# A two-layer encoder trunk on one core: keys that stay unnormalised until the block inverse, reordered transfers, and small matrix products spread over four tiles of TensorE

## The chip, the core and the metric

The kernel runs on one core of a Trainium2 chip. The core has TensorE (PE, matrix products into PSUM), VectorE (DVE), ScalarE (ACT), GpSimd (POOL) and a queue engine (SP); ACT and SP start transfers here. The metric is the device time of one execution in microseconds (us), as the median of several.

## What is computed

The input is one sequence of 1024 rows of 1024 float32 numbers. It passes an even layer (gated mixing and trailing means), a SwiGLU feed-forward block, an odd layer (RWKV-7 time mixing), a second SwiGLU block and a last norm. The part that the change touches most is the odd layer:

```python
r = xr @ w_r
k = xk @ w_k
kk = heads(k * k_k)                                  # 16 heads of 64
kk = kk / jnp.maximum(jnp.sqrt(jnp.sum(kk * kk, axis=-1, keepdims=True)), 1e-12)
...
y = wkv7_scan(rh, decay, kh, vh, -kk, kk * ah)       # a recurrence over the 1024 steps
...
def swiglu(hn, w_gate, w_up, w_down):
    return (jax.nn.silu(hn @ w_gate) * (hn @ w_up)) @ w_down
```

The recurrence multiplies a 64 by 64 state per head by its decay, adds a rank-one correction made of the normalised keys, and adds value times key.

## The kernel before, in words

**Numbers.** A dense product in float32 is made of three products of fp32r operands (high by high, high by low, low by high). Each weight block of 128 by 1024 is loaded by ACT's queue into `raw`, copied to `whi` by ACT and subtracted to `wlo` by DVE (L157 and L158, helper `split`); the three products are L399 to L401 (`mm3`). Small products are plain float32 and take two TensorE passes each.

**Halves.** The sequence is cut in two halves A and B of 512 columns (`h` = 0, 1), and a dense product streams 512 columns. The first layer and its feed-forward block run first. The gate and up products leave their hidden values in DRAM (`hid_d`), and the down products read them back (`hd`, L894). `down_steps` (L883) loads one group of two or three hidden blocks ahead; half A's groups alternate between a set of slots called `low` (tiles `ahi`, `alo`) and three slots `hd`. The residual of half A, `H[0]`, and of half B, `H[1]`, come back from `hm_d` (L1885, L1891).

**Projection, once for each half** (`project`, L1180). It runs over eight pairs of heads, p = 0 to 7. For each p: the key product, two low-rank products, the receptance product `r`, the square sums of the keys by four products with two columns (`norms`, into `bo`), a square root on POOL (`rsqrt`, L404), eight products that spread the result over the rows (`rb`, L1333), the keys times that (`kkn`, L1339), and from these the tiles `ar` and `bk` that go to DRAM. One p later `interact` (L1233) makes the 64 by 64 interactions of eight chunks, sixteen products (L1238); they go to DRAM, and after p = 3 and p = 7 a tile `iat` with 128 blocks of 32 by 32 comes back. `invert` (L1402) turns these into inverses in 31 steps on DVE, which are handed out five at a time between the other work. Gate values `g_d` are written from two tags of two buffers (L1212, L1214).

**Recurrence, once for each half** (`recur`, L1440), eight chunks of 64 steps, beside the dense products of a feed-forward block. For each chunk, `load` fetches `ar`, `bk`, `uv` and the inverse blocks `XT`; `gram` (products of `ar` with `bk`), `flip_bk` (transposes), `below` and `below2` (32 by 32 products that fill the lower block of the inverse), `own`, the product with `XT`, the state and the output follow. `bk` has one buffer, so the next chunk's load waits for `flip_bk`. All products of `recur` go through one helper, so most have line L1460.

**Order of the work.** Each engine runs its instructions in a fixed order, which the framework's scheduler sets by a simulated timeline; `drive` and `beside` set how side work is handed out between dense products, `tc.issue_after` puts one instruction behind another on its queue. A transfer on SP also waits until the transfer that used its completion semaphore before, some eight transfers back, has ended.

**The end.** Half A of the second block runs groups of hidden blocks `G1A`; after blocks 18 and 19 and their down products come the output projection of half B (`out_proj`), its norm, blocks 20 and 21, and then half B's feed-forward block.

Of the kernel before, what the change touches and what calls it, by code (L numbers as in the profile page):

```python
# [16 lines left out]
P = 128  # L17
# [11 lines left out]
LOWRANK_AT, GATE_AT, MIX_AT = (2, 8), (3, 8), (1, 2)  # L29
# [14 lines left out]
def tile_trunk(  # L44
# [309 lines left out]
    push_ffn(1, 0, G1A[2], push_act(("y", 1), y_d[1]))  # L354
    for e in push_o(1):
        e()
    push_ffn(1, 0, G1A[3])
# [525 lines left out]
    def down_steps(h, groups, wslot, hslot, ahead=True, after=None, between=iter(()), at={}, first={}):  # L883

        held = {}
# [4 lines left out]
        def load(g):  # L890
            for f in g:
                if f not in held:
                    held[f] = hslot(f)
                    sp.dma_start(held[f].bitcast(F32), hid_d[h][:, f])  # L894
# [38 lines left out]
    def ffn(l, h, hn, fp, groups=GROUPS, last=False, nd=3, after=None, between=iter(()), early=False):  # L933
# [3 lines left out]
        for kind, f in ffn_events(groups, early):  # L937
# [27 lines left out]
            else:  # L965
# [6 lines left out]
                for m in range(KT):  # L972
# [7 lines left out]
                    yield len(f) / 8  # L980

# [63 lines left out]
    xi_d = [dram.tile([2, 8, 2, 8, 32, 2, 32], F32, name=f"xi_d{h}") for h in range(2)]  # L1045
    at_d = [dram.tile([2, 8, 2, 8, 32, 32], F32, name=f"at_d{h}") for h in range(2)]
# [137 lines left out]
    def project(h, hn1, kp, ring, keep, before_v):  # L1184
# [21 lines left out]
        for m in range(KT):  # L1206
# [4 lines left out]
            t = tmp(("epx", "k")[m % 2], 2)  # L1211
# [21 lines left out]
        def interact(p, ar, bk):  # L1233

            oa = auxt()
            for c in range(8):
                for r in range(2):
                    pe.matmul(  # L1238
                        oa[rows[r], c * 64 : (c + 1) * 64], bk[rows[r], c, 0, :], ar[rows[r], c, 0, :],
                        start=True, stop=True,  # L1240
                    )
            at = tmp("kkn", 2)
            act.activation(at, oa, AF.Copy)
# [6 lines left out]
            if p % 4 == 3:  # L1250
                iat = tmp("iat", 1, [P, 32, 32])
                for q in range(2):
                    sp.dma_start(
                        iat[q * 64 : q * 64 + 64].rearrange("b s t -> b (s t)"),
                        at_d[h][q, p - 3 : p + 1].rearrange("p r c s t -> (p r c) (s t)"),
                    )
                return iat

        def bonus(p, kt, j):
            pe.matmul(  # L1260
                bo[:, j * 16 + 2 * p : j * 16 + 2 * p + 2], kt[:, j * P : (j + 1) * P], ind2, start=True, stop=True
            )

# [13 lines left out]
        for p in range(KT):  # L1277
# [32 lines left out]
            n2 = bo[:, 64 + 8 * p : 72 + 8 * p]  # L1310
            rn = tmp("rn", 2, [P, 4, 2, 8])[:, 0, 0, :]

            def norms(j):
                pe.matmul(n2[:, 2 * j : 2 * j + 2], sq[:, j * P : (j + 1) * P], ind2, start=True, stop=True)
                if j == 3:
                    dve.tensor_scalar(out=rn, in0=n2[:, 0:8], scalar1=1e-24, scalar2=None, op0=ALU.max)
                    rsqrt(rn)

            small = [lambda j=j: norms(j) for j in range(4)]
            if prev is not None:  # L1320
                small += [lambda j=j, pv=prev: bonus(pv[0], pv[3], j) for j in range(4)]
            if p:
                o = mmt()
                dense2(o, *take(("r", h, p)), xr, between=small)
            else:
                o = o_r
                for go in small:
                    go()
            invert_on(INV)
            rb = auxt()  # L1330
            for j in range(4):
                for r in range(2):
                    pe.matmul(  # L1333
                        rb[rows[r], j * P : (j + 1) * P], bc(rn[:, 2 * j + r : 2 * j + r + 1], [P, 64]), ident,
                        start=True, stop=True,
                    )
# [696 lines left out]
```

## Time and profile before

| what | value |
|---|---|
| median of 3 executions | 2438.87 us (2436.91 to 2441.32) |
| the profiled execution, its own time | 2432.77 us |
| span in its profile | 2431.1 us |
| mean granted TensorE clock | 0.987 |
| PE matmul busy | 2347.3 us, 97% |
| DVE busy | 1475.1 us, 61% |
| ACT busy | 937.1 us, 39% |
| POOL busy | 214.8 us, 9% |
| moved by DMA | 342.17 MB, 141 GB/s |

A group row of the profile reads: line, engine, operation, written tile and read tiles, shapes, count, busy time and the mean length of one, then the idle time of the engine just before the group and what ended it. Because matmuls are pipelined, the lengths of neighbours overlap: the busy time of a group divided by its count is what one pass really takes. A row of stretches gives, after the stretch, the busy time of each engine with its count, the granted clock, the share of the DMA engines and GB/s.

### The profile page before, as it was taken

The page shows a single profiled execution, that of the slowest core. Times are in us where ns is not written, and L with a number is a line of the kernel's source. Part 1 is how long each engine was busy: PE and PEld are TensorE (multiplying, and loading weights), DVE is VectorE, ACT ScalarE, POOL GpSimd, SP SyncE. Part 2 cuts the span into 40 slices and gives each one's busy share as a digit, 9 for nine tenths or more (in the row PEclk, how much of TensorE's full clock was granted, in tenths as well). Part 3 has the DMA queues.
Part 4 walks back from the last instruction along what each step waited for, and adds up shares of the span by engine and source line. Part 5 has one row for each costly group of instructions (what it writes and reads, how often), then busy time and mean ns, then how long its engine had stood idle before and what let it go on. Part 6 is the DMA issues. An engine that isn't in the chain of part 4 may idle for free. (4 is left out here: it accounts for less than half of the span.)

```text
span 2431.1 us, 38203 instructions
## 1 busy us (share of the span) xinstructions
PE 2347.3 (97%) x15567; PEld 1917.3 (79%) x15567; DVE 1475.1 (61%) x2328; ACT 937.1 (39%) x1403; POOL 214.8 (9%) x246
## 2 busy tenths in 40 slices
PE   8999999999899999999999999999999999999998
PEld 6888888888687878777777778777878788888887
DVE  6445765655567857856767947866664536444443
ACT  6233444444214753423335744433332224322223
POOL 0200000000000033201100123201100001000001
PEclk9999999999999999999999999999999999999999
DMA  5114443324665565775435465675544423433231
GB/s 179 52 52 147 152 152 96 121 96 165 226 233 172 171 163 133 207 202 167 143 117 168 150 169 142 190 232 159 146 121 132 123 77 97 144 98 96 86 105 52
DMA packets 406767, 342.17 MB, mean 141 GB/s; under 512 B 78080, under 2 KB 351616, under 8 KB 405824
## 3 DMA queue, kind: packets, MB, share of 16 engines
q10 hardware_dynamic: 266048, 195.33, 27.0%
q1 hardware_dynamic: 140544, 144.41, 19.1%
q8 instruction: 122, 2.00, 0.3%
q14 instruction: 53, 0.43, 0.1%
HBM read 263.07 MB, written 76.61 MB: 140 GB/s over the span
## 5 line engine op out<-in xcount | busy, mean ns | idle before, releaser
L399 PE MATMUL mm<-ahi,whi 128*128 128x512 f32 x1376 | 541.0, 394 | 7.0 <-ACT whi L157 3.0
L400 PE MATMUL mm<-alo,whi 128*128 128x512 f32 x1376 | 541.7, 394 | 2.6 <-DVE alo L158 2.5
L401 PE MATMUL mm<-ahi,wlo 128*128 128x512 f32 x1376 | 539.7, 392 | 1.6 <-DVE wlo L158 1.6
L157 ACT ACTIVATE whi<-raw 128x1024 fp32r<-128x1024 f32 (+1 forms) x280 | 282.1, 1014 | 572.2 <-PE mm L400 441.7
L158 DVE TENSOR_TENSOR wlo<-raw,whi 128x1024 fp32r<-128x1024 f32 (+1 forms) x280 | 328.5, 1177 | 249.8 <-ACT whi L157 231.5
L399 PEld LDWEIGHTS mm<-ahi,whi 128*128 128x128 f32 x1376 | 258.7, 188 | 66.2 <-ACT whi L157 4.7
L400 PEld LDWEIGHTS mm<-alo,whi 128*128 128x128 f32 x1376 | 258.8, 188 | 60.6 <-DVE alo L158 5.6
L401 PEld LDWEIGHTS mm<-ahi,wlo 128*128 128x128 f32 x1376 | 258.7, 188 | 57.9 <-DVE wlo L158 2.9
L493 DVE TENSOR_TENSOR h<-h,mm 128x512 f32<-128x512 f32 x276 | 185.8, 684 | 149.4 <-PE mm L401 148.4
L399 PE MATMUL mm<-hidhi,wdhi 128*128 128x512 f32 x304 | 118.4, 398 | 3.2 <-ACT hidhi L958 2.5
L400 PE MATMUL mm<-hidlo,wdhi 128*128 128x512 f32 x304 | 120.0, 395 | 0.0
L401 PE MATMUL mm<-hidhi,wdlo 128*128 128x512 f32 x304 | 119.7, 394 | 0.0
L730 PE MATMUL mm<-ahi,whi 128*128 128x512 f32 x296 | 115.6, 390 | 0.0
L731 PE MATMUL mm<-alo,whi 128*128 128x512 f32 x296 | 115.2, 389 | 0.0
L732 PE MATMUL mm<-ahi,wlo 128*128 128x512 f32 x296 | 113.6, 389 | 0.0
L955 DVE TENSOR_TENSOR sg<-sg,mm 128x512 f32<-128x512 f32 x52 | 35.7, 687 | 119.8 <-PE mm L401 119.6
L157 ACT ACTIVATE wdhi<-raw 128x1024 fp32r<-128x1024 f32 x42 | 43.3, 1056 | 160.2 <-PE mm L400 137.0
L399 PE MATMUL mm<-hd,dhi 128*128 128x512 f32 x192 | 75.9, 396 | 13.8 <-DMA hd<-hid_d 11.4
L400 PE MATMUL mm<-hd,dhi 128*128 128x512 f32 x192 | 75.8, 395 | 0.0
L401 PE MATMUL mm<-hd,dlo 128*128 128x512 f32 x192 | 74.9, 393 | 0.0
L399 PEld LDWEIGHTS mm<-hidhi,wdhi 128*128 128x128 f32 x304 | 57.7, 190 | 16.5 <-ACT hidhi L958 2.9
L400 PEld LDWEIGHTS mm<-hidlo,wdhi 128*128 128x128 f32 x304 | 57.9, 190 | 12.3 <-issue 0.5
(395 smaller groups left out, 4274.2 us busy)
## 6 DMA issues: line engine op xcount, KB each, us to landing
raw<-in_ffn_w_down_dram ACTq DMA_DIRECT2D x88, 512.0 KB
raw<-in_ffn_w_gate_dram ACTq DMA_DIRECT2D x74, 512.0 KB
raw<-in_ffn_w_up_dram ACTq DMA_DIRECT2D x74, 512.0 KB
hid_d<-hid SPq DMA_DIRECT2D x36, 512.0 KB
hd<-hid_d SPq DMA_DIRECT2D x26, 512.0 KB
raw<-in_ab_w_in_dram ACTq DMA_DIRECT2D x16, 512.0 KB
raw<-in_ab_w_out_dram ACTq DMA_DIRECT2D x16, 512.0 KB
raw<-in_rwkv_w_r_dram ACTq DMA_DIRECT2D x16, 512.0 KB
```

Of the source, the lines that this page charges most:

```text
L157: act.activation(hi, src, AF.Copy)
L158: (eng or dve).tensor_tensor(out=lo, in0=src, in1=hi.bitcast(F32), op=ALU.subtract)
L399: pe.matmul(o, whi, xhi, start=first, stop=False)
L400: pe.matmul(o, whi, xlo, start=False, stop=False)
L401: pe.matmul(o, wlo, xhi, start=False, stop=last)
L493: dve.tensor_tensor(out=H[h][:, m, :], in0=H[h][:, m, :], in1=o, op=ALU.add)
L730: pe.matmul(o, wh[:, k, :], x[0][:, k, :], start=st, stop=False, skip_group_check=True)
L731: pe.matmul(o, wh[:, k, :], x[1][:, k, :], start=False, stop=False, skip_group_check=True)
L732: pe.matmul(o, wl[:, k, :], x[0][:, k, :], start=False, stop=k == 3, skip_group_check=True)
L955: dve.tensor_tensor(out=s, in0=s, in1=o, op=ALU.mult)
```

## The change

1. **Keys.** `kkn` becomes the unnormalised key times its factor, one ACT copy with a scale. The root on POOL and the `rb` products are gone. The inverse square norms enter later: `sums` takes the square sums of four p from `bo`, transposes them (one product), writes them to `n2_d`, and `interact` reads them back into row 31 of `iat`, takes the reciprocal and multiplies the 31 other rows; `invert` starts from a diagonal of these numbers and not of ones.
2. **Four tiles.** `interact` sends odd chunks to the other half of the output rows and to a second PSUM bank, with two ACT copies for one. `below` and `below2` do the same with 32 by 32 products: pairs of odd p go to the other 32 columns. `w1` is one ACT copy for an ACT and a DVE copy, the copies to `XT` are four for two, and `load` fetches a small tile `xo` twice per chunk.
3. **Transfers.** In the first down products the hidden blocks of the next group come ahead of the rest of `H[0]` and `H[1]`, `hd` has four slots, and half B's groups are loaded ahead. `lnw` comes behind the keys of chunk 2. The state goes through DRAM between the halves. The gate values use four tags.
4. **Order.** Half B's low-rank product is taken at event 6 and not 8. At the end, groups 20 and 21 are joined with 18 and 19, so the gate product of block 20 comes ahead of the down products of 18 and 19.

```diff
-LOWRANK_AT, GATE_AT, MIX_AT = (2, 8), (3, 8), (1, 2)
+LOWRANK_AT, GATE_AT, MIX_AT = (2, 6), (3, 8), (1, 2)
...
                 wd = {f: take(("d", 0, h, f)) for f in g}
+                if ahead and gi + 1 < len(groups):
+                    load(groups[gi + 1])
                 if gi in at:
                     at[gi]()
-                if ahead and gi + 1 < len(groups):
-                    load(groups[gi + 1])
...
-            t = tmp(("epx", "k")[m % 2], 2)
+            t = tmp(("k", "epx", "av", "sg")[m % 4], 2)
...
-            oa = auxt()
+            oa = [auxt() for _ in range(2)]
             for c in range(8):
+                e, i = c % 2, c // 2
                 for r in range(2):
                     pe.matmul(
-                        oa[rows[r], c * 64 : (c + 1) * 64], bk[rows[r], c, 0, :], ar[rows[r], c, 0, :],
+                        oa[e][rows[r ^ e], i * 64 : (i + 1) * 64], bk[rows[r], c, 0, :], ar[rows[r], c, 0, :],
...
+                dve.tensor_scalar(out=d2, in0=d2, scalar1=1e-24, scalar2=None, op0=ALU.max)
+                dve.reciprocal(d2, d2)
+                dve.tensor_tensor(out=iat[:, 0:31], in0=iat[:, 0:31], in1=bc(d2.unsqueeze(1), [P, 31, 32]), op=ALU.mult)
...
+        def sums(p):
+
+            rn = tmp("rn", 1, [P, 64])[:, :32]
...
+            ot = auxt()
+            pe.transpose(ot[:32, :P], rn, ident)
+            t = nt.tile([P, HT], F32, tag="nsq", bufs=2, name="n2")[:32, :P]
+            act.activation(t, ot[:32, :P], AF.Copy)
+            for q in range(2):
+                sp.dma_start(
+                    n2_d[h][q, p - 3 : p + 1].rearrange("p r (j c) t -> (p r j) c t", c=2),
...
-            rb = auxt()
-            for j in range(4):
-                for r in range(2):
-                    pe.matmul(
-                        rb[rows[r], j * P : (j + 1) * P], bc(rn[:, 2 * j + r : 2 * j + r + 1], [P, 64]), ident,
-                        start=True, stop=True,
-                    )
...
-            dve.scalar_tensor_tensor(out=kkn, in0=kt, scalar=col(C_KK + p), in1=rb, op0=ALU.mult, op1=ALU.mult)
+            act.activation(kkn, kt, AF.Copy, scale=col(C_KK + p))
...
-        pool.memset(xf[:, 0:2048:65], 1.0)
+        dve.tensor_copy(xf[:, 0:2048:65], iat[:, 31, :])
...
+                sp.dma_start(xo[b0 : b0 + 32], x2[:, 1::2, :])
+                loaded[0] = sp.dma_start(XT[b0 + 32 : b0 + 64, :, 32:64], x2)
...
             for p in range(8):
                 for r in (1, 0):
+                    b0, o0 = r * 64, r * 64 + 32 * (1 - p % 2)
+                    mm(
+                        ow[o0 : o0 + 32, p // 2, 0:32], gt[b0 : b0 + 32, p, r, 32:64], x1[b0 : b0 + 32, p, :],
+                        start=True, stop=True, tile_position=(b0, o0),
+                    )
...
-                    with tc.issue_after(loaded[0].ins):
+                    with tc.issue_after(loaded[0].ins), tc.issue_after(keys[0].ins):
...
-    wslot, hslot = slots_of(f, 4, 3)
+    wslot, hslot = slots_of(f, 4, 4)
...
-    for k in range(4, KT, 2):
-        a_loaded = sp.dma_start(H[0][:, k : k + 2, :], hm_d[0][:, k : k + 2, :])
...
+    def rest_a():
+        for k in range(4, KT, 2):
+            with tc.issue_after(hid_loads[-1]):
+                sp.dma_start(H[0][:, k : k + 2, :], hm_d[0][:, k : k + 2, :])
...
-    drive(ffn(1, 0, hnA, f, G1A[2], between=take_act(("y", 1)), early=True))
-    exhaust(out_proj(1, ys))
-    hnB = norm_split(1, C_FFN + 8, b)
-    drive(ffn(1, 0, hnA, f, G1A[3], last=True, early=True))
+    drive(ffn(1, 0, hnA, f, G1A[2] + G1A[3], last=True, between=take_act(("y", 1)), early=True, then={G1A[2][0][-1]: out_b}))
```

On SP, at the passage from the first block's gate and up products to half A's down products, before (`hid_d` ends in 77 for half A and 78 for half B, `h<-hm_d_75` is `H[0]`, `h<-hm_d_76` is `H[1]`, `hd` is the second group):

```order
L743 DMA hid_d_77<-hid 128x1024
L743 DMA hid_d_78<-hid 128x1024
L1885 DMA h<-hm_d_75 128x1024 x2
L1891 DMA h<-hm_d_76 128x1024 x4
L894 DMA hd<-hid_d_77 128x1024 x3
L894 DMA ahi<-hid_d_77 128x1024
L894 DMA alo<-hid_d_77 128x1024
```

And at the same place of the changed kernel:

```order
L747 DMA hid_d_77<-hid 128x1024
L747 DMA hid_d_78<-hid 128x1024
L898 DMA hd<-hid_d_77 128x1024 x3
L1913 DMA h<-hm_d_75 128x1024 x2
L898 DMA hd<-hid_d_77 128x1024
L898 DMA ahi<-hid_d_77 128x1024
L898 DMA alo<-hid_d_77 128x1024
L1926 DMA h<-hm_d_76 128x1024 x2
L898 DMA hd<-hid_d_77 128x1024 x2
```

The three `hd` loads of the second group moved from behind six loads of `h` to the front of them.

On SP, at the start of half A's recurrence, before (from the residual of half B, `h`, by way of the second chunk's `ar`, `uv` and, for each half of the rows, two loads into `XT`, to its `bk`):

```order
L1791 DMA h<-h_d_86 128x1024 x4
L1475 DMA ar<-ar_d_1974 128x1024
L1480 DMA uv<-v_d_1978 64x512
L1481 DMA uv<-v_d_1978 64x512
L1487 DMA XT<-xi_d_1984 32x8x64
L1490 DMA XT<-xi_d_1984 32x8x32
L1487 DMA XT<-xi_d_1984 32x8x64
L1490 DMA XT<-xi_d_1984 32x8x32
L1477 DMA bk<-bk_d_1976 128x1024
```

And in the changed kernel:

```order
L1820 DMA h<-h_d_86 128x1024 x4
L1495 DMA ar<-ar_d_1974 128x1024
L1500 DMA uv<-v_d_1978 64x512
L1501 DMA uv<-v_d_1978 64x512
L1508 DMA XT<-xi_d_1984 32x8x64
L1511 DMA xo<-xi_d_1984 32x4x32
L1512 DMA XT<-xi_d_1984 32x8x32
L1508 DMA XT<-xi_d_1984 32x8x64
L1511 DMA xo<-xi_d_1984 32x4x32
L1512 DMA XT<-xi_d_1984 32x8x32
L1497 DMA bk<-bk_d_1976 128x1024
```

The second chunk's `bk` stands where it stood, with two `xo` loads more ahead of it, and two more in the first chunk's loads.

On PE, in half A's projection, at the end of a receptance product, before (`kkn` squares and `k` bonus sums go into `bo`, `rn` is what the `rb` products spread):

```order
L400 MATMUL mm<-xlo,whi 128x512
L401 MATMUL mm<-xhi,wlo 128x512
L1260 MATMUL bo<-ind_6460,k 128x2 x4
L1333 MATMUL aux<-ident,rn 64x128 x8
L399 MATMUL mm<-xhi,whi 128x512
```

And in the changed kernel:

```order
L404 MATMUL mm<-alo,whi 128x512
L405 MATMUL mm<-ahi,wlo 128x512
L1349 MATMUL bo<-ind_6461,kkn 128x2 x4
L1276 MATMUL bo<-ind_6461,k 128x2 x4
L403 MATMUL mm<-xhi,whi 128x512
```

The eight `rn` rows are gone, and the two groups of four products into `bo`, which stood some twenty dense products apart, stand together.

More of the change, by code (lines that the diff above doesn't have):

```diff
@@ L353, in tile_trunk @@
     push_ffn(1, 0, G1A[1])
[L354 to L357, printed above, removed]
+    y1, o1 = push_act(("y", 1), y_d[1]), push_o(1)
+    for i, e in enumerate(e for e in ffn_events(G1A[2] + G1A[3], True) if e[0] != "d"):
+        if e == ("u", G1A[3][0][0]):
+            for go in o1:
+                go()
+        push_ffn_event(1, 0, *e)
+        if e[0] in "gu":
+            next(y1, None)
     push_ffn(1, 1)
@@ L881, in full_steps, with down_steps @@
             yield 0.5
-    def down_steps(h, groups, wslot, hslot, ahead=True, after=None, between=iter(()), at={}, first={}):
-        held = {}
+    def down_steps(h, groups, wslot, hslot, ahead=True, after=None, between=iter(()), at={}, first={}, loaded=None):
+        held, loaded = {}, [] if loaded is None else loaded
         for g in groups:
@@ L930, in slots_of, with ffn @@
         )
-    def ffn(l, h, hn, fp, groups=GROUPS, last=False, nd=3, after=None, between=iter(()), early=False):
+    def ffn(l, h, hn, fp, groups=GROUPS, last=False, nd=3, after=None, between=iter(()), early=False, then={}):
         dests["d"] = lambda: (fp.tile([P, D], F32R, tag="wdhi", bufs=nd, name="wdhi"),
@@ L1242, in interact @@
             at = tmp("kkn", 2)
-            act.activation(at, oa, AF.Copy)
+            for e in range(2):
+                act.activation(c64(at)[:, e::2, :], c64(oa[e][:, :256]), AF.Copy)
             for r in range(2):
@@ L1309, in project @@
             pool.tensor_copy(pct[:, h * 8 : h * 8 + 8, p], c64(epx)[:, :, 63])
[L1310 to L1321, printed above, removed]
+            n2 = bo[:, 64 + 8 * p : 72 + 8 * p].rearrange("t (r j) -> t r j", j=4)
+            o = o_r
             if p:
                 o = mmt()
[L1324 to L1328, printed above, removed]
-            invert_on(INV)
-            rb = auxt()
-            for j in range(4):
-                for r in range(2):
-                    pe.matmul(
-                        rb[rows[r], j * P : (j + 1) * P], bc(rn[:, 2 * j + r : 2 * j + r + 1], [P, 64]), ident,
-                        start=True, stop=True,
-                    )
+                dense2(o, *take(("r", h, p)), xr)
+            for j in range(4):
+                pe.matmul(n2[:, :, j], sq[:, j * P : (j + 1) * P], ind2, start=True, stop=True)
+            if prev is not None:
+                for j in range(4):
+                    bonus(prev[0], prev[3], j)
+            if p % 4 == 3:
+                sums(p)
+            invert_on(INV)
             ar, bk = tmp("ar", 2, [P, 8, 2, 64]), tmp("bk", 2, [P, 8, 2, 64])
             kkn = tmp("kkn", 2)
-            dve.scalar_tensor_tensor(out=kkn, in0=kt, scalar=col(C_KK + p), in1=rb, op0=ALU.mult, op1=ALU.mult)
+            act.activation(kkn, kt, AF.Copy, scale=col(C_KK + p))
             dve.scalar_tensor_tensor(
@@ L1452, in recur @@
         lnw = wt("lnw", 1, [P, 8, 64])
[L1453 to L1454 removed]
+        C, ypair, loaded, keys = {}, [], [None], [None]
+        S, Q, last = [wt("S", 2, [P, 8, 64])], {}, []
+        if h == 0:
+            pool.memset(S[0], 0.0)
         def ordered(f, *args, **kw):
@@ L1476, in load @@
             bk = wt("bk", 1, [P, 8, 2, 64])
-            sp.dma_start(bk, bk_d[h][c])
+            keys[0] = sp.dma_start(bk, bk_d[h][c])
             uv = wt("uv", 2, [P, 2, 8, 64])
```

89 lines of the change are left out of this document (54 added, 35 removed).

## Prediction

> **What bounds the kernel now.** The first thing to read is the head of the page and the engine shares.
>
> ```profile
> span 2431.1 us, 38203 instructions
> PE 2347.3 (97%) x15567; PEld 1917.3 (79%) x15567; DVE 1475.1 (61%) x2328; ACT 937.1 (39%) x1403; POOL 214.8 (9%) x246
> ```
>
> TensorE is busy for 2347.3 of 2431.1 us. No other engine comes near that over the whole, so a change can win in two ways only: by fewer or shorter TensorE passes, or out of the 83.8 us in which TensorE does nothing. The second view is the table of waits of TensorE, which says who ended that idle time (sum, number, longest):
>
> ```profile
> PE mm L399 <- DMA hd<-hid_d: 11.4, 2, 9.8
> PE sm L1460 <- DMA bk<-bk_d: 8.8, 4, 6.0
> PE aux L1238 <- DVE bk L1351: 3.3, 2, 2.3
> PE mm L399 <- ACT epx L1212: 2.8, 2, 1.5
> PE mm L399 <- ACT hidhi L958: 2.5, 1, 2.5
> PE bo L1260 <- DVE rn L1316: 2.3, 2, 1.5
> PE sm L1462 <- DMA bk<-bk_d: 2.1, 1, 2.1
> PE mm L399 <- ACT k L1212: 1.2, 1, 1.2
> PE aux L1333 <- POOL rn L404: 0.7, 2, 0.3
> ```
>
> The third view is the clock in 50 us stretches. The columns are the stretch and its length, then busy time and count of PE, PEld, DVE, ACT and POOL, then the granted clock, the DMA share and GB/s.
>
> ```profile
> 600.00:650.00 50.00, 39.56 (x165) 31.96 (x164) 21.00 (x28) 10.34 (x13) 0.12 (x1) 0.90 0.64 244
> 900.00:950.00 50.00, 48.23 (x340) 40.30 (x339) 31.55 (x53) 20.61 (x30) 17.32 (x18) 0.95 0.56 145
> 950.00:1000.00 50.00, 47.96 (x314) 38.51 (x313) 46.10 (x82) 24.98 (x38) 17.59 (x14) 0.88 0.51 141
> 1050.00:1100.00 50.00, 44.02 (x584) 35.50 (x584) 23.30 (x40) 11.72 (x18) 0.61 (x2) 0.93 0.84 226
> 1400.00:1450.00 50.00, 46.88 (x287) 37.83 (x288) 23.63 (x31) 26.93 (x40) 13.04 (x17) 0.97 0.62 171
> 1500.00:1550.00 50.00, 44.91 (x320) 36.26 (x319) 46.59 (x85) 25.10 (x38) 22.22 (x15) 0.97 0.53 142
> 1900.00:1950.00 50.00, 45.67 (x192) 36.47 (x191) 25.62 (x31) 13.10 (x16) 0.00 (x0) 0.97 0.39 116
> ```
>
> Each of these stretches holds one of the waits above, and the clock is below 1 there: a gap costs its own length and some passes at a lower clock behind it. In 950 to 1000, where half A's projection runs beside the block inverse, DVE is busy for 46.10 of 50 us; that matters below.
>
> **The change part by part.** The small products come first, since they are sure to run. Their groups (count | busy, mean ns of one pass):
>
> ```profile
> L1333 PE MATMUL aux<-ident,rn 128*64 128x128 f32 x256 | 18.7, 292 | 0.7 <-POOL rn L404 0.7
> L1238 PE MATMUL aux<-ar,bk 64*64 64x64 f32 x512 | 18.4, 221 | 3.4 <-DVE bk L1351 3.3
> L1460 PE MATMUL sm<-XT,w 32*32 32x32 f32 x512 | 11.1, 192 | 0.0
> L1460 PE MATMUL sm<-XT,gt 32*32 32x32 f32 x512 | 11.1, 192 | 0.0
> ```
>
> *The spread of the norms* (L1333) goes: 18.7 us. Neighbours overlap its ends a little, and four transposes of two passes each come in; I take -17 us.
>
> *The interactions* (L1238) take 18.4 / 512 = 36 ns a pass on two tiles, one per row half. What four tiles give is shown by `own`, which runs 64 by 64 products on all four:
>
> ```profile
> 1100.29 0.22 PE L1460 MATMUL sm<-uv,gt 64*64 64x64 f32 x1
> 1100.30 0.22 PE L1460 MATMUL sm<-S,ar 64*64 64x64 f32 x1
> 1100.31 0.22 PE L1460 MATMUL sm<-uv,gt 64*64 64x64 f32 x1
> 1100.31 0.22 PE L1460 MATMUL sm<-S,ar 64*64 64x64 f32 x1
> 1100.35 0.22 PE L1460 MATMUL sm<-uv,gt 64*64 64x64 f32 x1
> ```
>
> Four passes start in 0.06 us, 15 ns each. So 512 passes save 512 x (36 - 15) = 10.8 us; the ends of each of 16 series don't shrink, and I take -9.5 (bounds -8 and -11).
>
> *The 32 by 32 products* (`below`, `below2`) take 22 ns a pass on two tiles, 1024 passes. No row shows 32 by 32 on four tiles. One end is no gain, if 22 ns were the issue of a pass; the other is half, -11 us. The rows above show passes starting 10 ns apart, less than 22, so I lean to the far end: -8 us. The Trainium skill speaks against this part: TensorEngine Tiling (Array Packing), section Instruction Overhead, states about 60 cycles of overhead per matmul, so that one column costs what sixty do, and warns against tiling a dimension that is small already. By it this part would save nothing; the 15 ns of `own` lie below the 25 ns that 60 cycles make at the 2.4 GHz of the Trainium skill (an estimate), so the trace does not bear it out for 64 columns, and no row shows it for 32 columns on four tiles.
>
> *The hidden blocks* at the passage to the down products. Before, SP issues six `h` loads of 0.5 MB and then the three `hd` that TensorE needs next:
>
> ```profile
> 621.62 0.79 SPq L1885 DMA_DIRECT2D h<-hm_d  x2
> 622.51 1.89 SPq L1891 DMA_DIRECT2D h<-hm_d  x4
> 624.45 2.75 SPq L894 DMA_DIRECT2D hd<-hid_d  x3
> 636.69 0.76 PE L399 MATMUL mm<-hd,dhi 128*128 128x512 f32 x1 [9.75 <-DMA hd<-hid_d]
> 640.66 0.44 PE L399 MATMUL mm<-hd,dhi 128*128 128x512 f32 x1
> 640.94 0.39 PE L400 MATMUL mm<-hd,dhi 128*128 128x512 f32 x1
> 641.17 0.40 PE L401 MATMUL mm<-hd,dlo 128*128 128x512 f32 x1
> ```
>
> TensorE stands 9.75 us, then makes nine passes in 640.66 - 636.69 = 3.97 us that take 9 x 0.23 = 2.07 later: 11.65 us in all. Now the `hd` go first. From the first `h` at 621.62 to the pass at 636.69 nine blocks of 0.5 MB landed, 1.67 us each; three would land at 621.62 + 5.0 = 626.6, when TensorE gets there (636.69 - 9.75 = 626.94). What is late next are the last two `h` loads, two blocks behind, at 630; PSUM has five buffers here and holds the sums until then. I take -10.5 (bounds -5 and -11.65).
>
> *The projection's waits.* The chain from the square sums by POOL's root and the spread to `kkn` on DVE goes, so the keys wait for ACT alone. The waits on `bk`, `rn` (DVE) and `rn` (POOL) are 3.3 + 2.3 + 0.7 = 6.3 us. The clock lost in 900 to 1000 and in 1500 to 1550 is (0.05 + 0.12 + 0.03) x 50 = 10 us. If all went, that would be -16. But DVE is the cover that runs out:
>
> ```profile
> L1339 DVE SCALAR_TENSOR_TENSOR kkn<-k,vec,aux 128x512 f32<-128x512 f32 x16 | 11.9, 742 | 24.9 <-PE aux L1333 24.9
> ```
>
> Three p fall in 950 to 1000, so moving `kkn` to ACT takes 3 x 0.74 = 2.2 us from DVE's 46.10, to which the start of each inverse adds a scaled copy of 992 elements and three short operations. ACT, 24.98 of 50 busy there, takes the copy over. DVE still needs some 44 of those 50 us, so this stretch can shrink by 6 at most, and 3 x (18.7 + 9.5) / 16 = 5 of that are the passes counted above. I take -4 for the two halves, bounds +3 and -16. The way of the norms through DRAM hides: `sums` comes before the interactions of its p, whose own way through DRAM is as long.
>
> *Gate values.* Waits on `epx` and `k` of L1212, 2.8 + 1.2 = 4.0, and (1 - 0.97) x 50 = 1.5 us of clock in 1400 to 1450; twice the buffers: -4 (0 to -5.5).
>
> *The join at the end.* The wait on `hidhi` is 2.5 and the clock in 1900 to 1950 costs 1.5; the gate product of block 20 now stands in it: -4 (0 to -4).
>
> *The starts of the recurrences.* `bk` waits are 8.8 + 2.1 = 10.9 us, 6.0 of them one gap, with (1 - 0.93) x 50 = 3.5 us of clock behind it:
>
> ```profile
> 1073.71 0.30 SPq L1490 DMA_DIRECT2D XT<-xi_d  x1
> 1075.76 0.34 SPq L1477 DMA_DIRECT2D bk<-bk_d  x1
> 1080.32 1.08 PE L1460 MATMUL sm<-ar,bk 64*64 64x128 f32 x13 [5.98 <-DMA bk<-bk_d]
> ```
>
> Here SP issues `bk` 2.0 us behind a small load. Putting `lnw` behind `bk` helps later chunks, about -2; but four `xo` loads now stand ahead of this `bk` on the same queue. TensorE has some dense products more before it gets there. Sum 0 (bounds -10 and +6).
>
> *The rest.* The copies to `XT` and `w1` lie on ACT and DVE beside dense products. The state's way through DRAM and the low-rank product at event 6 move work by a few us under dense products: 0, bounds plus and minus 2. In the new order some bursts of the recurrence have one dense product, or none, where there were six between the product with `XT` and the state: these will wait for copies of `uv`. I take +5 (0 to +10).
>
> Sum: -17 - 9.5 - 8 - 10.5 - 4 - 4 - 4 + 0 + 5 = -52 us. Against the profiled execution, 2432.8 us by its own time (span 2431.1), that is 2381; it was 6 below the median, and against the median of 2438.9 the forecast is 2387 us.
>
> **The rivals.**
> - *Passes only.* What is freed of waits comes back as other waits, above all on DVE in the projection and at the recurrences. For it speaks the stretch with DVE at 46.10; against it that the `hd` gap is a matter of queue order alone. Without the four terms of 10.5, 4, 4 and 4 the sum is -29.5: 2409 us. Chance 0.2.
> - *The issue of a pass binds.* If 22 ns is what a pass costs however many tiles there are, `below` gives 0 for -8, and the interactions go from 36 to 22, 7 for 9.5: -41.5, 2397 us. This is the rule of the Trainium skill named above. The 15 ns of `own` speak against it; that no 32 by 32 series is denser than 22 speaks for it. Chance 0.1.
> - *The recurrence starts well.* If the dense products ahead of the second chunk's `bk` outlast its loading, the 6.0 us gap with its 3.5 us of clock goes, and in the projection half of the 16 instead of 4: -52 - 9.5 - 4 = -65.5, or -70 with the order costing nothing: 2369 us. Chance 0.13.
> - *Slower: `xo` holds the queue.* In each of 16 chunks two small loads now come ahead of the next `bk` on SP. Where the queue is full they cost 2.0 us each, by the rows above: 16 x 4 = 64 us if TensorE waits for all of it, -52 + 64 = +12, 2451 us. It decides from the point where a chunk's slack before `gram` is less than 4 us. Against it are the loads of a later chunk, 0.48 us apart:
>
> ```profile
> 1107.98 0.42 SPq L1490 DMA_DIRECT2D XT<-xi_d  x1
> 1108.46 0.44 SPq L1487 DMA_DIRECT2D XT<-xi_d  x1
> ```
>
>   Chance 0.05. DMA: Bandwidth & Descriptors in the Trainium skill, section Why small descriptors are slow, says that short descriptors pay a fixed part each; the pieces of `xo` are 128 bytes.
>
> **How the numbers follow.** The forecast has 0.52: 2387 us, by itself 2375 to 2399. The rivals have 0.2 (2409), 0.1 (2397), 0.13 (2369) and 0.05 (2451). The range from 2365 to 2411 takes in all but the last and the tails, in which several bounds fall on one side. About 0.2%, 5 us, is what a measurement of this kernel can tell from no change. Faster by more than that: 0.52 + 0.2 + 0.1 + 0.13 less a little for tails, 0.93; slower 0.05; the same 0.02.
>
> **What would show it.** Right: no L1333 group; the interactions at 15 to 20 ns a pass by busy time over count; the two 32 by 32 groups near 14; no wait on `hd` above 2 us and a clock near 1 in 600 to 650; no waits on `rn`. DVE near its limit in the second part of each projection, with waits of L1238's successor on `bk` left, would show the cover that ran out. Wrong: PE busy falls by 30 us and the span doesn't (a wait took its place, and the table of waits names it), 32 by 32 groups still at 22 ns, or `bk` waits well above 11 us with `xo` ahead of them.

## The result, and the profile after

The changed kernel takes 2414.9 us in the median of five runs (2412.4 to 2427.6) beside 2437.5 for the kernel before (2433.9 to 2441.3): ratio 0.9931, 95% interval 0.9913 to 0.9949. By that ratio, which is used from here on, it is 17 us faster; 52 were forecast (2387, range 2365 to 2411). The two medians are 22.6 us apart; in the runs below the kernel before took 2432.3 to 2434.1 us. The profiled execution took 2418.3 us by its own time, span 2416.5, 14.6 less than before's.

The page of the changed kernel, its head and engine shares:

```profile
span 2416.5 us, 37755 instructions
PE 2325.2 (96%) x15315; PEld 1897.8 (79%) x15315; DVE 1466.9 (61%) x2312; ACT 948.3 (39%) x1467; POOL 178.5 (7%) x226
```

TensorE is busy 22 us less than before, and its idle time has grown from 83.8 to 91.3 us. The groups of the small products (count | busy, mean ns of one | idle time ahead):

```profile
L1246 PE MATMUL aux<-ar,bk 64*64 64x64 f32 x512 | 12.6, 227 | 8.5 <-DVE bk L1370 8.5
L1480 PE MATMUL sm<-XT,gt 32*32 32x32 f32 x512 | 7.3, 195 | 0.0
L1480 PE MATMUL sm<-xo,w 32*32 32x32 f32 x256 | 7.0, 194 | 0.0
L1480 PE MATMUL sm<-XT,w 32*32 32x32 f32 x256 | 7.0, 194 | 0.0
L1288 PE MATMUL aux<-ident,rn 128*32 128x128 f32 x4 | 1.1, 278 | 2.6 <-ACT rn L1286 2.6
```

The passes got shorter as planned. The spread of the norms (18.7 us) is gone for 1.1 us of transposes; the interactions fell from 18.4 to 12.6 us; the 32 by 32 products from 22.2 to 14.3 (the two halves of the second product run side by side, so 7.0 counts once). From the first start to the last end, a series of 32 passes takes 0.63 us for 1.08 in the interactions and 0.38 for 0.62 in the 32 by 32 products; the last pass starts 0.48 us behind the first for 0.93, and 0.26 for 0.50. In 16 and 32 such series that is 15 us of passes.

The waits of TensorE that bear on the change (sum, number, longest):

```profile
PE sm L1480 <- DVE gt L1529: 8.7, 5, 3.6
PE aux L1246 <- DVE bk L1370: 8.5, 6, 2.0
PE sm L1480 <- DMA bk<-bk_d: 8.4, 2, 7.4
PE mm L403 <- ACT whi L157: 6.4, 3, 4.0
PE sm L1480 <- issue: 4.3, 3, 2.9
PE mm L403 <- ACT hidhi L962: 3.2, 2, 2.9
PE aux L1288 <- ACT rn L1286: 2.6, 2, 1.3
PE sm L1482 <- DMA xo<-xi_d: 1.9, 1, 1.9
PE sm L1482 <- DMA bk<-bk_d: 1.8, 1, 1.8
PE mm L403 <- ACT k L1219: 0.8, 1, 0.8
```

The wait on `hd` is gone, that on the gate values is 0.8 for 4.0, and the two on `rn` by POOL and VectorE (3.0 together) are gone. In their place the interactions wait 8.5 us for VectorE's `bk` (3.3 before), the new transposes wait 2.6 us for ACT's `rn`, and `gt`, `xo`, `whi` and "issue" are new or larger. The loads of `bk` hold TensorE as long as before, 10.2 us for 10.9.

Where that tells is seen when the span is cut at the same four events in both kernels: first and last small sum into `bo` of half A's projection, the same of half B's, and the end. Columns: stretch and length, busy time and count of PE, PEld, DVE, ACT and POOL, granted clock, DMA share, GB/s. Before:

```profile
868.78:1005.04 136.26, 132.38 (x905) 108.81 (x904) 100.89 (x172) 60.94 (x91) 48.27 (x46) 0.94 0.54 144
1005.04:1422.28 417.24, 391.88 (x3982) 311.61 (x3981) 297.63 (x538) 184.86 (x287) 36.74 (x42) 0.98 0.57 168
1422.28:1555.72 133.44, 126.68 (x906) 104.36 (x905) 99.92 (x172) 60.93 (x91) 51.50 (x46) 0.99 0.54 139
1555.72:2423.07 867.35, 854.13 (x6055) 702.48 (x6053) 445.49 (x692) 270.41 (x391) 39.61 (x40) 1.00 0.41 122
```

After:

```profile
853.61:976.18 122.57, 116.76 (x780) 95.30 (x779) 96.33 (x161) 66.87 (x115) 31.61 (x36) 0.97 0.61 154
976.18:1401.86 425.68, 394.54 (x3981) 314.28 (x3979) 296.55 (x540) 182.56 (x295) 36.05 (x42) 0.97 0.56 167
1401.86:1527.09 125.23, 116.74 (x781) 95.15 (x780) 95.84 (x159) 67.86 (x115) 32.27 (x38) 0.97 0.59 152
1527.09:2408.72 881.63, 856.62 (x6052) 703.53 (x6050) 447.41 (x699) 270.42 (x399) 39.42 (x39) 0.98 0.41 121
```

Up to the first projection 15.2 us are won, in the projections 13.7 and 8.2. The second and fourth stretch, with the recurrences, hold the same passes as before (3982 and 3981, 6055 and 6052), and those of them that got shorter should make each 4 us shorter: they are 8.4 and 14.3 us longer. So 37 us were won and 23 lost again, with a lower clock (0.98 to 0.97, 1.00 to 0.98).

The `hd` gap of before is closed; the first product starts 9.4 us earlier, without a wait:

```profile
627.28 0.39 PE L403 MATMUL mm<-hd,dhi 128*128 128x512 f32 x1
```

### The profile page after: what moved, and what is told of

The parts are those of the page before. It is cut to its first block, busy times and chain, and to the rows that moved or that the text cites. A ratio compares the mean times of both kernels' runs of the same rounds, so it can differ in the third digit from the quotient of the medians.

```text
span 2416.5 us, 37755 instructions
## 1 busy us (share of the span) xinstructions
PE 2325.2 (96%) x15315; PEld 1897.8 (79%) x15315; DVE 1466.9 (61%) x2312; ACT 948.3 (39%) x1467; POOL 178.5 (7%) x226
## 5 line engine op out<-in xcount | busy, mean ns | idle before, releaser
L403 PE MATMUL mm<-ahi,whi 128*128 128x512 f32 x1376 | 542.9, 396 | 10.5 <-ACT whi L157 6.0
L157 ACT ACTIVATE whi<-raw 128x1024 fp32r<-128x1024 f32 (+2 forms) x284 | 286.4, 1014 | 513.7 <-PE mm L404 384.7
L158 DVE TENSOR_TENSOR wlo<-raw,whi 128x1024 fp32r<-128x1024 f32 (+2 forms) x284 | 338.4, 1195 | 228.8 <-ACT whi L157 210.2
L158 DVE TENSOR_TENSOR wdlo<-raw,wdhi 128x1024 fp32r<-128x1024 f32 x42 | 52.8, 1259 | 26.6 <-ACT wdhi L157 26.2
L405 PEld LDWEIGHTS mm<-hidhi,wdlo 128*128 128x128 f32 x304 | 58.2, 192 | 12.8 <-issue 0.7
L403 PE MATMUL mm<-xhi,whi 128*128 128x512 f32 (+1 forms) x160 | 65.3, 408 | 0.0
```

The source lines that it names most:

```text
L157: act.activation(hi, src, AF.Copy)
L158: (eng or dve).tensor_tensor(out=lo, in0=src, in1=hi.bitcast(F32), op=ALU.subtract)
L403: pe.matmul(o, whi, xhi, start=first, stop=False)
L405: pe.matmul(o, wlo, xhi, start=False, stop=last)
```

## The experiments

The theory after the first reading had three parts: the loads of `xo` hold up SP's queue; the joined end costs time; and the new order puts too few dense passes between dependent small products ("thin bursts"). Its rival was that the shorter passes are on the path and the loss is elsewhere. Ratios are to the kernel before, which ran again beside each group of runs, with 95% intervals; 0.1% is 2.4 us. The difference of two ratios is uncertain by some 4 to 6 us. No run puts the old keys, hidden blocks or gate values back, so what these are worth is read from the traces alone.

**xo_copy**: `xo` made on the chip.

```
-                sp.dma_start(xo[b0 : b0 + 32], x2[:, 1::2, :])
+                pool.tensor_copy(xo[b0 : b0 + 32], XT[b0 + 32 : b0 + 64, 1::2, 32:64])
```

> The changed kernel, but the copies of the lower inverse blocks for odd pairs (xo) are no longer loaded on SP's queue: GpSimd copies them on the chip from XT. TensorE's order in half A's recurrence stays what it is in the changed kernel (408 dense passes between its first and last small product). Theory 'thin bursts' (too few dense passes between dependent small products): half A's recurrence keeps its waits of about 16.7 us, and the whole is within 3 us of the changed kernel, ratio to the kernel before 0.992 to 0.994. Theory 'queue' (xo loads hold up bk): the waits on xo (1.9 us) and bk at the start of half B's recurrence (7.4 us) fall below 2 together and some of those in half A go too, so about 9 us less than the changed kernel, ratio about 0.989.

Measured 0.9901 (0.9887 to 0.9915): 7 us less than the changed kernel, near the number of "queue", with intervals that just touch. The waits did not go as "queue" said. At the start of half B's recurrence TensorE still waits 3.0 and 3.8 us for `bk` (1.9 for `xo` and 7.4 for `bk` in the changed kernel), half A's waits for `bk` grow from 2.8 to 4.7, and all waits for `bk` and `xo` together go from 12.1 to 11.5 us only. What the loads do to SP's queue is seen at the start of half B's recurrence. In the changed kernel:

```profile
1587.76 0.53 SPq L1508 DMA_DIRECT2D XT<-xi_d  x1
1588.34 0.65 SPq L1511 DMA_DIRECT2D xo<-xi_d  x1
1593.67 0.30 SPq L1512 DMA_DIRECT2D XT<-xi_d  x1
...
1596.90 0.43 SPq L1495 DMA_DIRECT2D ar<-ar_d  x1
1610.70 0.39 SPq L1497 DMA_DIRECT2D bk<-bk_d  x1
```

With `xo` copied:

```profile
1581.46 0.53 SPq L1508 DMA_DIRECT2D XT<-xi_d  x1
1584.16 0.30 SPq L1511 DMA_DIRECT2D XT<-xi_d  x1
...
1590.13 0.44 SPq L1495 DMA_DIRECT2D ar<-ar_d  x1
1601.31 0.34 SPq L1497 DMA_DIRECT2D bk<-bk_d  x1
```

From its first issue to its last, the first chunk's series of six small loads takes 5.9 us, that of four 2.7; from the second chunk's `ar` to its `bk`, for which TensorE stood 7.4 us, it is 13.8 us and 11.2. One such issue lasts 0.3 to 0.7 us; between them SP waits until earlier transfers have ended (from 1575 to 1620 the loads into `XT` and `xo` waited 4.3 us for `ar` and 5.7 for `h`). So the delay in the queue is shown, but not that it makes up all of the 7 us: the order of half B's recurrence changed too, with 452 dense passes in it for 466. In four_alone and four_copy below, which differ in the same way and have equal numbers of dense passes in both recurrences, copying `xo` wins 4 us.

**split_end**: the changed kernel with the last blocks of half A split as before.

```
-    drive(ffn(1, 0, hnA, f, G1A[2] + G1A[3], last=True, ..., then={G1A[2][0][-1]: out_b}))
+    drive(ffn(1, 0, hnA, f, G1A[2], between=take_act(("y", 1)), early=True))
+    exhaust(out_proj(1, ys))
+    hnB = norm_split(1, C_FFN + 8, b)
+    drive(ffn(1, 0, hnA, f, G1A[3], last=True, early=True))
```

> The changed kernel with the last blocks of half A's feed-forward part split again as before (the join taken back). TensorE's order up to there doesn't change. If the join saves the wait on the last hidden block, as forecast (4 us): +4 us against the changed kernel, ratio 0.995. If the join is what lost time at the end (the waits of 2.9 us on hidhi at 1912 and of 4.0 us on a weight block at 2050): -5 us, ratio 0.991. If it does nothing: within 1.5 us.

Measured 0.9915 (0.9899 to 0.9931), 4 us less than the changed kernel, though the intervals overlap. One wait stands for it:

```profile
2054.68 0.80 PE L403 MATMUL mm<-ahi,whi 128*128 128x512 f32 x1 [3.95 <-ACT whi L157]
```

All five kernels of this study with the join have such a wait between 2041 and 2064 us (3.8 to 4.1 us); none with the split end has one of over 1 us there. The wait on `hidhi`, for which the forecast credited the join, is there either way (2.9 and 2.6 us, 2.5 before).

**xo_split**: both edits together.

> The changed kernel with xo copied on the chip by GpSimd and the end split as before: both edits of the first runs together. If they are independent, 7 us (queue) and 3 to 4 us (the wait of 3.8 us on a weight block at the end, which the split doesn't have) add up: ratio 0.986 to 0.988. If one order accident is only replaced by another: 0.990 or above.

Measured 0.9869 (0.9856 to 0.9881): 32 us less than before, 15 less than the changed kernel; the intervals of both pairs (with xo_copy and with split_end) are apart. With xte below it is the fastest kernel of this study that does the whole work. Its second and fourth stretch:

```profile
977.31:1394.45 417.14, 388.09 (x3980) 308.92 (x3979) 297.06 (x540) 180.84 (x292) 41.30 (x56) 0.99 0.56 169
1520.51:2389.67 869.16, 852.68 (x6052) 700.64 (x6050) 446.30 (x696) 269.66 (x399) 44.92 (x55) 0.99 0.41 122
```

They are as long as before's (417.24 and 867.35). So the two costs are out, and the 8 us of shorter 32 by 32 passes still don't show.

**four_alone** and **four_copy**: the kernel before with the four-tile products alone (`interact`, `below`, `below2`, the loads to them), with `xo` loaded and copied.

> The kernel before with only the interactions and the 32 by 32 products laid over four tiles, xo loads included. By the passes alone (7 us of interactions, 7.7 of 32 by 32 products): -15 us, ratio 0.994. Theory 'thin bursts': the order is thinned as in the changed kernel (419 dense passes in half A's recurrence where there were 461, 471 in half B's where there were 494), which gives back 8 us in each recurrence: -3 to +3 us, ratio 0.999 to 1.001. Theory 'queue': 9 us come back at one place, -6 us, and the waits elsewhere stay as before.

> The kernel before with both groups on four tiles, as in the run four_alone, but xo is copied on the chip instead of loaded; TensorE's order is the same in both. If the loss of four_alone (7 us slower than before) comes from the small loads of xo on the queue, this is back at the kernel before or under it: ratio 0.995 to 1.000. If it comes from the thinner order and from stalls without any wait that the profile shows (14.7 us of issue in four_alone, 0 before): ratio 1.000 to 1.004, with more than 8 us of issue left in the table of waits.

Measured 1.0029 (1.0016 to 1.0042) and 1.0012 (1.0004 to 1.0021). Four tiles alone make this kernel slower, with 15 us less of passes: in four_copy the interactions take 11.1 us for 18.4, the 32 by 32 products 14.8 for 22.2. Its table of waits shows where that went:

```profile
PE sm L1462 <- DMA bk<-bk_d: 16.1, 5, 5.6
PE aux L1335 <- POOL rn L404: 6.2, 2, 3.1
PE sm L1464 <- DMA bk<-bk_d: 2.8, 2, 2.5
```

The waits on `bk` in the recurrences are 18.9 us for 10.9 before, and the spread of the norms waits 6.2 us for POOL's root where it waited 0.7. That is 13.5 us more of waiting, in the two stages whose passes got shorter, as if TensorE only came there earlier and stood for the same loads and the same root. (The order changed with the passes, to 419 and 471 dense passes in the two recurrences for 461 and 494, so the two are not told apart here.) In four_alone the waits on `rn` are 6.2 as well, and "issue" is 14.7. "Issue" falls to 2.5 us in four_copy, but that is only a name: the same two gaps of half B stand in both, first four_alone, then four_copy:

```profile
1636.73 0.66 PE L1462 MATMUL sm<-ar,bk 64*64 64x128 f32 x2 [4.68 <-issue]
1663.00 1.30 PE L1462 MATMUL sm<-ar,bk 64*64 64x128 f32 x17 [4.74 <-issue]
```

```profile
1633.32 0.66 PE L1462 MATMUL sm<-ar,bk 64*64 64x128 f32 x2 [3.53 <-DMA bk<-bk_d]
1657.79 2.10 PE L1462 MATMUL sm<-ar,bk 64*64 64x128 f32 x32 [4.13 <-DMA bk<-bk_d]
```

**inter2**, **two32**, **no_four**, **nofour_split**: the changed kernel with the interactions alone, the 32 by 32 products alone, or both on two tiles; the last with the end split too.

> The changed kernel with the interactions alone back on two tiles (the 32 by 32 products stay on four, xo is loaded). Their passes take 7 us more in the two projections. If VectorE sets the pace there (waits of 8.5 us on bk), TensorE's longer passes fall into those waits: 0 to +3 us against the changed kernel, ratio 0.993 to 0.9945. If the forecast's view holds that they pay nearly in full: +7 us, ratio 0.996.

> The changed kernel with the 32 by 32 products laid over two tiles as before (no xo). Their passes take 7.7 us more. Theory 'thin bursts': TensorE's order gets 480 dense passes into half A's recurrence (408 in the changed kernel, 461 before), its waits fall from 16.7 to about 10 us and the clock there from 0.97 back to 0.99, so the 7.7 us are paid back in full: 0 to -6 us against the changed kernel, ratio 0.990 to 0.993. Theory 'queue': the 9 us of bk and xo at half B's start go, but half A's waits stay near 16: about -1 us. Neither: +7.7 us, ratio 0.996.

> The changed kernel with both groups of small products, the interactions and the 32 by 32 products, back on two tiles and without xo: only the keys and the order of transfers and events are changed. Four tiles alone cost the kernel before 7 us where its passes were 15 us shorter. If that holds here too (four tiles are a loss whatever stands around them), this kernel is 5 to 10 us faster than the changed kernel: ratio 0.989 to 0.991. If the four tiles pay in the new order what their passes save, less the xo wait: +5 to +10 us, ratio 0.995 to 0.997.

> The kernel no_four (keys and order changed, both groups of small products on two tiles, no xo) with the end split as before. It stands to xo_split as two tiles to four, with the two known costs of the changed kernel (the loads of xo, the join at the end) taken out of both. If the 15 us of shorter passes arrive once those costs are gone, this is 10 to 15 us slower than xo_split: ratio 0.991 to 0.993. If neither group's passes arrive (VectorE sets the projections, the copies and loads set the recurrences): within 3 us of xo_split, ratio 0.986 to 0.988. The join alone should take it 4 to 8 us below no_four (0.9914).

Measured: inter2 0.9947 (0.9934 to 0.996), two32 0.9949 (0.9931 to 0.9968), no_four 0.9914 (0.9901 to 0.9928), nofour_split 0.9879 (0.986 to 0.9898). Beside the changed kernel, each group taken back alone costs 4 us and both taken back together win 4, each within its interval; that no_four is 8 us faster than either is clear of it, so the two groups have no prices that add up. The nearest pair is nofour_split and xo_split, 2.4 us apart with an interval of about 6: of the 15 us of passes little more than half can arrive. (xo_split also pays for GpSimd's copies of `xo`, which nofour_split doesn't need.) The projections of nofour_split:

```profile
852.29:971.81 119.52, 116.19 (x781) 96.08 (x780) 93.69 (x157) 65.84 (x106) 31.57 (x36) 1.00 0.60 155
1394.73:1518.28 123.55, 117.89 (x781) 97.31 (x779) 94.72 (x158) 68.31 (x109) 32.96 (x39) 0.99 0.59 152
```

With the longer interactions they are no longer than the changed kernel's 122.57 and 125.23 or xo_split's 125.00 and 126.06. There the four tiles bring nothing.

**xte** and **w1dve**: neutral edits of xo_split (which engine makes which small copy) that change the order.

```
-    act.activation(XT[0:32, e::2, ...], ...); dve.tensor_copy(XT[64:96, e::2, ...], ...)
+    for r0 in (0, 64): (act.activation if e else dve.tensor_copy)(XT[r0 : r0 + 32, e::2, ...], ...)
```

> The kernel xo_split with one neutral change: of the four small copies into XT per chunk, ScalarE makes the two of the odd pairs and VectorE the two of the even pairs, where each made one row half before. The work is the same, but TensorE's order differs: 444 dense passes in half A's recurrence where xo_split has 408, 466 in half B's for 452. Theory 'thin bursts': half A's recurrence loses about 4 us of its waits of 13 and some half clock, 3 to 6 us in all, ratio 0.984 to 0.986. If the number of dense passes between small products doesn't matter: within 1.5 us of xo_split, ratio 0.987.

> The kernel xo_split with the copy of w1 (128 by 128, 0.26 us, one per chunk) on VectorE instead of ScalarE: a second neutral change with a thicker order, 444 dense passes in half A's recurrence and 466 in half B's. Theory 'thin bursts': as for xte, 3 to 6 us less than xo_split, ratio 0.984 to 0.986. If the dense passes between don't matter: within 1.5 us of xo_split, or slower by the copies that now queue behind VectorE's.

Measured 0.987 (0.985 to 0.989) and 0.9879 (0.986 to 0.9898) beside 0.9869. "Thin bursts" falls: the order is thicker (444 and 466 dense passes in the two recurrences of both, 408 and 452 in xo_split) and the time the same. In xte's profile the second stretch is 412.4 us (417.1 in xo_split), the fourth 874.9 (869.2). A recurrence can move by 5 us either way with the order, but the number of dense passes in it doesn't say which.

**no_kav**, **kav**, **two_kav**, **kem**, **kem_two**: who sets the projections. Each is xo_split with one product of VectorE left out (no_kav) or on GpSimd (kav; kem with another, off the chain); two_kav and kem_two have the small products on two tiles (in two_kav only the 32 by 32).

```
-            dve.tensor_tensor(out=kt, in0=kt, in1=av, op=ALU.mult)
+            pool.tensor_tensor(out=kt, in0=kt, in1=av, op=ALU.mult)
...
-            dve.tensor_tensor(out=bk[:, :, 1, :], in0=c64(kt), in1=c64(em), op=ALU.mult)
+            pool.tensor_tensor(out=bk[:, :, 1, :], in0=c64(kt), in1=c64(em), op=ALU.mult)
```

> The kernel xo_split with the product of the keys and the gate in the projections left out altogether (16 products of 0.68 us on VectorE; the keys then go on without that factor). In kav the same product went to GpSimd and the projections got longer (129.7 and 124.5 us for 125.0 and 126.1), with twice the waits on bk. If VectorE's total sets the pace of the second part: each projection 2 to 4 us shorter than in xo_split, waits on bk below 5 us in all for 7.0. If the chain from the keys through GpSimd's other product to bk sets it: projections within 1 us of xo_split, waits on bk 6 to 7 us.

> The kernel xo_split with the product of the keys and the gate (k times av, 128 by 512, 0.68 us on VectorE, 8 per half) moved from VectorE to GpSimd. Theory 'VectorE sets the pace of the second part of each projection': the waits on bk (7.0 us in all) fall below 4 and each projection gets 2 to 4 us shorter, although GpSimd takes about 1.4 us for each. Its order is thick as well (455 and 500 dense passes in the recurrences, 408 and 452 in xo_split), which by 'thin bursts' is worth another 4 to 8 us: ratio 0.981 to 0.984. Rival: the chain through GpSimd to bk sets the pace; then the waits on bk grow by 0.7 us for each of some 8 keys and the projections get longer by 3 us each.

> The kernel kav, but with the 32 by 32 products on two tiles. Both have thick orders (here 461 and 527 dense passes in the recurrences, there 455 and 500). If four tiles for the 32 by 32 products pay their 7.7 us of passes once the order is not thinned by them, this is 5 to 9 us slower than kav. If their gain is always taken back, whatever the order: within 2 us of kav.

> The kernel xo_split with the product of the keys and the decay (k times em, 16 of 0.68 us on VectorE) moved to GpSimd; it fills the second half of bk, which is stored for the recurrence and which no interaction reads, so the chain to the interactions doesn't get longer as it did in kav. The bonus product is written to another tile so that VectorE doesn't wait for GpSimd. If VectorE's total sets the pace of the projections: each gets 2 to 6 us shorter (no_kav, which left out as much, gained 4 and 8 us up to the recurrences), waits on bk by interactions below 5 us for 7.0, ratio 0.982 to 0.985. If GpSimd's product is late at the store of bk and the recurrence waits for that: the gain goes at the first bk of each recurrence, within 2 us of xo_split.

> The kernel kem with both groups of small products on two tiles and without xo. With VectorE relieved, if the interactions and the 32 by 32 products on four tiles now pay what their passes save, this is 8 to 15 us slower than kem. If VectorE and the copies still set the pace: within 4 us, as nofour_split and xo_split are (0.9879 and 0.9869).

Measured: no_kav 0.9836 (0.9821 to 0.9852), kav 0.9929 (0.9906 to 0.9953), two_kav 0.9937 (0.9923 to 0.9951), kem 0.9904 (0.9889 to 0.9919), kem_two 0.992 (0.9907 to 0.9933). The second part of half A's projection in xo_split has VectorE busy for 49.09 of 52 us:

```profile
925.00:977.00 52.00, 47.31 (x294) 37.65 (x294) 49.09 (x91) 29.72 (x51) 14.28 (x12) 0.93 0.52 141
```

In no_kav 61 passes move behind the last sum, 32 of them short interactions, so the stretch between the sums doesn't compare. From the first sum to the first product of the recurrence it is, in xo_split and then in no_kav:

```profile
852.31:1038.94 186.63, 178.33 (x1050) 145.98 (x1048) 140.57 (x248) 91.49 (x144) 36.30 (x45) 0.97 0.64 179
1394.45:1589.21 194.76, 182.01 (x1069) 149.30 (x1068) 143.56 (x252) 95.13 (x148) 36.01 (x44) 0.97 0.65 177
```

```profile
852.20:1035.03 182.83, 173.35 (x1045) 141.88 (x1044) 131.63 (x239) 89.26 (x141) 34.78 (x44) 1.00 0.67 183
1391.23:1577.73 186.50, 175.46 (x1051) 144.11 (x1049) 135.81 (x242) 92.13 (x144) 32.96 (x41) 0.98 0.66 180
```

These are 3.8 and 8.3 us less, of which 4 and 19 dense passes of 0.227 us that moved out make 0.9 and 4.3. So eight products of 0.68 us, 5.4 us, bring 3 to 4 us in each half; the whole is 8 us shorter, and the interactions' waits on `bk` fall from 7.0 to 3.9. VectorE's work is on the path of the projections, though not microsecond for microsecond. On GpSimd the same product is no relief (129.7 and 124.5 us between the sums in kav for 125.0 and 126.1, waits on `bk` 14.0). kem's projections are 3.4 and 3.7 us shorter between the sums, but 16 dense passes, 3.6 us, moved out of each, and TensorE then waits 4.4 and 7.0 us for the first `bk` (1.4 and 3.9 in xo_split): its relief isn't seen either. kem_two and two_kav stand 4 and 2 us above their partners, within the intervals: again most of the passes' gain doesn't arrive.

**start**: xo_split with the first `ar` and `bk` of each recurrence on ScalarE's queue.

> The kernel xo_split with the first chunk's ar and bk of each recurrence loaded on ScalarE's queue instead of SP's, where they stand behind the store of the last block inverse, which waits for VectorE. TensorE's order in half A's recurrence doesn't change. If the start of the recurrence waits for that queue: the waits of 1.4 and 3.9 us on the first bk go, 4 to 7 us with the clock behind them, ratio 0.984 to 0.985. If it waits for the block inverse itself (by way of the product below): the wait only moves to the first 32 by 32 product, within 1.5 us of xo_split.

Measured 0.9886 (0.9873 to 0.99), 4 us slower than xo_split, with intervals that overlap. TensorE waits 2.1 and 4.5 us for the first `bk` instead of 1.4 and 3.9, so standing in SP's queue was not what held these loads.

## Why the prediction was off, by its own steps

The steps that failed are the two terms of shorter passes, counted in full as time won (17.5 us, where the pairs of runs show 2 to 4, within their intervals), and two more: `xo`, put at nothing, and the join, which had the wrong sign.

- *The spread, -17*, and *the hidden blocks, -10.5*: right in mechanism, as far as the traces tell. The group is gone; `hd` starts 9.4 us earlier, without a wait.
- *Gate values, -4*: waits of 0.8 for 4.0.
- *The interactions, -9.5*: the size is too large. It took the 15 ns between two starts in `own` from 36 ns, which is busy time over count and holds the end of each series. By starts it was 30 ns before and 15 after, 7.2 us in 16 series; by busy time 36 and 25 ns, 5.8 us. The step that failed is that they were counted on the path. The text had VectorE at 46.10 of 50 us and wrote that the stretch could shrink by 6 at most; it still credited the passes in full and 4 us of waits on top. The projections gave 21.9 us for a forecast 30.5, and inter2 and nofour_split show as short ones with two tiles. The cover that runs out was seen and not charged.
- *The projection's waits, -4*: wrong in sign. The 6.3 us of before (`bk` and the two on `rn`) became 8.5 on `bk` and 2.6 on ACT's `rn`.
- *The 32 by 32 products, -8*: the size of the passes is right, 14 ns by busy time over count for 22, and 8 for 16 from start to start. The Trainium skill's rule against it (TensorEngine Tiling (Array Packing), section Instruction Overhead, about 60 cycles a matmul) is not borne out for the start of one pass after another here: 32 passes start within 0.26 us. But three pairs (xo_split with nofour_split, kem with kem_two, kav with two_kav) show 2 to 4 us, within their intervals, for 8 to 15 us of passes. The forecast took TensorE as what ends the waits in the recurrence. It waits for loads there too: in four_copy 7.4 us of shorter 32 by 32 passes come with 8.0 us more of waiting for `bk`.
- *The recurrence starts, 0 (bounds -10 and +6)*: `xo` costs 4 us (four_alone against four_copy), 7 (xo_copy) or 11 (xo_split against split_end). The delay that the rival "`xo` holds the queue" named is seen in SP's queue, at a few places instead of all sixteen chunks; that it makes up the whole cost is not shown.
- *The join, -4*: wrong in sign. It is +4 (split_end), +8 (xo_split against xo_copy) or +9 (nofour_split against no_four): the wait it was to remove stayed, and one of 3.95 us came 140 us later. That the weight loads come late there because output rows take their buffers was only argued, from the code.
- *Tighter order, +5*: the idea that fewer dense passes cost time fell with xte and w1dve.

Put together: -52, plus 9.5 and about 6 for passes that didn't arrive, plus 8 for the join, plus 7 for `xo`, is -21; measured -17. Without `xo` and the join it is -52 + 9.5 + 6 + 4 = -32, and xo_split measured -32. These sums were made afterwards, and the other terms stand in them as forecast. The rival nearest to the result was "passes only" (2409), right that waits come back in the projection and the recurrences, wrong that the passes arrive.

Still open is what sets the recurrences' length. The second stretch came out at 412 to 430 us under nearly the same work (no_kav's 433 holds 61 passes more), and neither the number of dense passes nor the passes' length accounts for it. Of the 8.5 us by which it is longer in the changed kernel than in xo_split, 6.4 are busy time of TensorE, for 3981 and 3980 passes at a clock of 0.97 and 0.99, and 2.1 are idle time.

## What to carry to other kernels

Credit a shorter pass only in stages where TensorE's own end is what the next step waits for; in a stage where another engine is busy nine tenths of the time, credit at most what that engine gets rid of. Count small loads on an in-order queue by the large load that stands behind them, and undo a change in parts before keeping it: here two of its parts cost 15 of the 32 us that the rest of it won.

## What the runs showed of the hardware

A product on GpSimd holds VectorE up when VectorE reads both its inputs from SBUF. In xo_split, VectorE first, then GpSimd:

```profile
925.82 0.39 DVE L1428 TENSOR_TENSOR it<-iat,xi 128x220 f32<-128x220 f32 x1
927.15 0.68 DVE L1370 TENSOR_TENSOR ar<-mm,epx 128x512 f32<-128x512 f32 x1
927.75 1.22 DVE L1428 TENSOR_TENSOR it<-iat,xi 128x231 f32<-128x231 f32 x1
```

```profile
927.42 1.29 POOL L1362 TENSOR_TENSOR kkn<-kkn,av 128x512 f32<-128x512 f32 x1
```

The same kind of product takes 1.22 us instead of 0.39 and ends just after GpSimd's; the one that reads `mm` from PSUM keeps its 0.68 us. Over the whole of xo_split, 12 instructions `wlo<-raw,whi` beside a GpSimd product take 2.03 us in the median for 1.23 alone, and 12 `ar<-mm,epx` take 0.68 either way. The Trainium skill, SBUF — State Buffer, section SBUF: two separate sides, says that the two engines lock a shared port pair for a whole instruction, VectorE when it has two SBUF inputs; the trace agrees. It bears on why work moved to GpSimd was no relief: VectorE's instructions beside a GpSimd product are longer than their like alone by 15 us in all in xo_split, 29 in kav and 22 in kem (estimates, each against the median of its kind), and each move took 10.9 us from VectorE.

The clock can fall after gaps of some 2 us. In the changed kernel, with the row of the stretch that follows:

```profile
1354.22 0.50 PE L403 MATMUL mm<-ahi,whi 128*128 128x512 f32 x1 [2.06 <-ACT whi L157]
1355.82 0.80 PE L405 MATMUL mm<-ahi,wlo 128*128 128x512 f32 x1 [0.86 <-DVE wlo L158]
1354.95:1361.77 6.82, 5.96 (x15) 4.70 (x15) 6.15 (x8) 4.25 (x7) 0.00 (x0) 0.50 0.60 174
```

After 2.06 and 0.86 us of idle time the granted clock is 0.50, and 12 passes start 0.43 us apart instead of 0.23, from 1356.41 to 1361.53: 2.4 us more. Here the gaps cost nearly twice their length. Not every gap does: behind one of 1.68 us at 1482.14 the passes start 0.23 us apart.
